# Three of the last quarter's four down units by seven block products, with adding DMAs for side and weight sums

## The chip, the cores and the metric

The kernel runs on one core of a Trainium2 chip. A core has a matrix engine (TensorE, PE in the profile; its weight loads are listed as PEld), a vector engine (VectorE, DVE), a scalar engine (ScalarE, ACT), a general engine (GpSimd, POOL) and SyncE (SP), which issues most DMAs. Matrix products are accumulated in PSUM, which has eight banks of 128 x 512 float32 numbers; everything else lies in SBUF, 128 partitions wide. The metric is device microseconds of one execution, lower is better.

## The reference, cut to what matters

Two layers, each with a token mixer, an MLP with a squared ReLU, and a gated embedding. All is float32; SEQ is 512, D_MODEL 1024, D_FF 4096. The change touches the MLP alone:

```python
for i in range(DEPTH):
    hn = rmsnorm(h, norm_mix_g[i])
    h = h + mixer(hn, ...)                                   # even or odd layout
    hn = rmsnorm(h, norm_mlp_g[i])
    u = jnp.square(jax.nn.relu(hn @ w_mlp_up[i]))            # 512 x 4096
    h = h + u @ w_mlp_down[i]                                # 512 x 1024
    gate = jax.nn.sigmoid(rmsnorm(h, norm_ple_g[i]) @ w_ple_gate[i])
    h = h + (p[i] @ w_ple_proj[i]) * gate
return rmsnorm(h, final_norm_g)
```

## The kernel before

**Layout.** The hidden state is kept transposed, as eight tiles `h[0..7]` of 128 features x 512 tokens. Each float32 operand of a product is split into a high half in TensorE's reduced float32 format (float32r) and a low half that holds the rest; `mm3` (line 137) makes one product of three matmuls, high x high, low x high, high x low. A split is one copy on ScalarE (`wh`, `uh`, `hi`) and one subtraction on VectorE (`wl`, `ul`, `lo`).

**Order.** The code names engines and data, and a scheduling layer fixes each engine's order of instructions when the program is built, from its own estimates of when things are ready; it puts in the semaphores. At run time every engine follows its list strictly, so an instruction that waits holds up all that stand behind it on its engine. Each DMA that SP or POOL issues stands in that engine's list in the same way.

**The MLP.** `mlp` (line 704) cuts the 4096 hidden columns into four quarters (`ch`), and each quarter into four up units and four down units (`c`). An up unit, `up(ch, c)`, loads 1 MB of weights (`raw`, two buffers), splits them, makes two 128 x 512 products (48 matmuls of 512 columns), multiplies by the norm's factor and clips at zero on VectorE (line 720), squares on ScalarE (line 721), and splits the result. The result `u` holds the four blocks B11, B12 (under the name T3), B21, B22: two tiles of hidden columns by two halves of 256 tokens.

A down unit, `down(ch, c)`, makes the two tiles `h[2c]`, `h[2c+1]` from the quarter's 1024 hidden columns. For quarters 0 to 2 it works by Strassen's scheme in Winograd's form: the 2 x 2 blocks of weights and of activations are first summed (`T1`, `T2`, `T3`, `T4` from u in lines 724 to 729; the weight sums in lines 742 to 745, on VectorE), and seven block products take the place of eight: 7 x 4 x 3 = 84 matmuls of 256 columns. The weights arrive packed block by block (`_pack4`). Three of the seven products are added into `h` directly; the four others go to two side tiles per unit, `sides[c][0..1]`, which collect over the quarters; `side_sums(c)` (line 788) then adds them into `h` by eight VectorE additions of 256 columns.

The last quarter is different. Its up units split only the four plain blocks, and its four down units, `down_last(c)` (line 798), are classical: 48 matmuls of 512 columns each, one PSUM tile per output tile. `side_sums` stands between the last up units, ahead of all of them. When a `down_last` unit has added its tile, `nxt.done(k)` (class `Norm`, line 230) splits `h[k]` for the gate's product and adds its square into the running sum of the next norm (line 247, VectorE).

**Around it.** After the MLP the gate stage starts (`ple_t` in layer 0, `ple_final` in layer 1); its first unit takes `h[0]` to `h[7]` in this order, and `ple_final` also transposes `h` back (line 858) and copies the result out of PSUM on VectorE (line 859). POOL has no work in the MLP.

The functions that the change touches follow.

Of the kernel before, what the change touches and what calls it, by code (L numbers as in the profile page):

```python
# [19 lines left out]
P = 128  # L20
# [42 lines left out]
def trunk(  # L63
# [139 lines left out]
    sbmask = const([P, P], "sbmask", F32R)  # L203
    nc.vector.tensor_copy(sbmask, mask)
    ident_r = const([P, P], "ident_r", F32R)
    nc.vector.tensor_copy(ident_r, ident)


# [21 lines left out]
    class Norm:  # L230
        def __init__(self, kind, layer):
            self.kind, self.layer, self.hl, self.acc = kind, layer, {}, None

        def done(self, k, stats=True):
            self.hl[k] = split_tile(h[k], gcol(self.kind, self.layer, k))
            if stats:
                self.stats(k)

        def stats(self, k, after=()):
            sq = t2k("e" if self.acc else "rstd")  # L240
# [461 lines left out]
    def mlp(layer, fpool, norm, nxt):  # L702
        ahl = norm.parts()
        rstd = []
        NCH = 4
        sides = [[fpool.tile([P, S], F32, tag=f"side{x}{c}", name=nm("side"), bufs=1) for x in range(2)] for c in range(4)]
        hidden = {}

        def up(ch, c):
            blk = block(w_up[layer, 4 * ch + c], KT, P)  # L710
            accs = [ps_wide() for _ in range(2)]
            run(lin_units(accs, blk, ahl, 0, KT, ch == 0 and c == 0))
            if not rstd:
                rstd.append(norm.finish(use_tables(sig_tail) if layer == 0 else None))
            u = fpool.tile([P, 7, HW], F32, tag="u", name=nm("u"), bufs=1)
            uh = fpool.tile([P, 7, HW], F32R, tag="uh", name=nm("uh"), bufs=5)
# [5 lines left out]
            parts = slice(0, 7)  # L722
            if ch < NCH - 1:
                nc.vector.tensor_tensor(
                    u[:, T1:T3 + 1:2], u[:, B11:B22 + 1:3], u[:, T3:T3 + 1].to_broadcast([P, 2, HW]), op=ALU.subtract)
                nc.vector.scalar_tensor_tensor(
                    u[:, T2], u[:, T1], -1.0, u[:, B22], op0=ALU.mult, op1=ALU.subtract)
                nc.vector.scalar_tensor_tensor(  # L728
                    u[:, T4], u[:, T2], -1.0, u[:, B21], op0=ALU.mult, op1=ALU.subtract)
            else:  # L730
                parts = slice(B11, B22 + 1)
            nc.scalar.activation(uh[:, parts], u[:, parts], AF.Copy)  # L732
            nc.vector.tensor_tensor(ul[:, parts], u[:, parts], uh[:, parts].bitcast(F32), op=ALU.subtract)  # L733
            hidden[ch, c] = (uh, ul)

        def down(ch, c):
            raw = wload(w_down[layer, 4 * ch + c])
            rv = raw.rearrange("p (s k c) -> p s (k c)", s=4, k=4)
            A12, A22, S3, A11 = range(4)
            sums = fpool.tile([P, 3, S], F32, tag="sums", name=nm("sums"), bufs=1)  # L740
            S1, S2, S4 = range(3)
            nc.vector.tensor_tensor(sums[:, S1], rv[:, S3], rv[:, A22], op=ALU.add)
            nc.vector.tensor_tensor(sums[:, S2], sums[:, S1], rv[:, A11], op=ALU.add)
            nc.vector.tensor_tensor(rv[:, S3], rv[:, S3], rv[:, A11], op=ALU.add)
            nc.vector.tensor_tensor(sums[:, S4], sums[:, S2], rv[:, A12], op=ALU.add)

            def split(src):
                n = src.shape[1]
                if n == 2:
                    hi, lo = (wpool.tile([P, 2, 4, P], F32R, tag=t, name=nm(t), bufs=3) for t in ("wh", "wl"))  # L750
                else:
                    hi, lo = (t2k("e", dtype=F32R).rearrange("p (s k c) -> p s k c", s=1, k=4) for _ in range(2))
                src = src.rearrange("p s (k c) -> p s k c", k=4)
                nc.scalar.activation(hi, src, AF.Copy)  # L754
                nc.vector.tensor_tensor(lo, src, hi.bitcast(F32), op=ALU.subtract)
# [5 lines left out]
            def product(bank, half, w, x, t, start, stop):  # L761
                wh, wl = w
                acc = banks[bank][:, half * HW:half * HW + HW]
                for k, (uh, ul) in enumerate(us):
                    mm3(acc, wh[:, x, k], wl[:, x, k], uh[:, t], ul[:, t], start and k == 0, stop and k == 3)

            def total(x, bank):
                if ch == 0:
                    nc.scalar.activation(sides[c][x], banks[bank], AF.Copy)
                else:  # L770
                    nc.vector.tensor_tensor(sides[c][x], sides[c][x], banks[bank], op=ALU.add)

            w = split(sums[:, S1:S2 + 1])
            product(0, 0, w, 0, T1, True, False)
            product(0, 1, w, 1, T2, False, True)
            total(0, 0)
            w = split(rv[:, S3:A11 + 1])
            product(1, 0, w, 0, T3, True, False)
            product(1, 1, w, 1, B11, False, True)
            total(1, 1)  # L780
            product(2, 1, split(sums[:, S4:S4 + 1]), 0, B22, True, False)
            w = split(rv[:, A12:A22 + 1])
            product(2, 0, w, 0, B21, False, True)
            nc.vector.tensor_tensor(h[2 * c], h[2 * c], banks[2], op=ALU.add)
# [3 lines left out]
        def side_sums(c):  # L788
            left, right = slice(0, HW), slice(HW, S)
            (s1t1, s2t2), (s3t3, a11b11) = ((x[:, left], x[:, right]) for x in sides[c])  # L790
            h11, h12, h21, h22 = (h[2 * c + i][:, x] for i in range(2) for x in (left, right))
            for dst, x, op in ((h11, a11b11, ALU.add), (s2t2, a11b11, ALU.add), (h12, s2t2, ALU.add), (s3t3, s2t2, ALU.add),
                               (h21, s3t3, ALU.subtract), (h12, s1t1, ALU.add), (s3t3, s1t1, ALU.add),
                               (h22, s3t3, ALU.subtract)):
                nc.vector.tensor_tensor(dst, dst, x, op=op)

        def down_last(c):
            blk = block(w_down[layer, 4 * (NCH - 1) + c], KT, P)
            uhl = [tuple(x[:, B11 + 2 * i:B11 + 2 * i + 2].rearrange("p a c -> p (a c)") for x in hidden[NCH - 1, k])
                   for k in range(4) for i in range(2)]  # L800
            for i in range(2):
                acc = ps_wide()
                lin(acc, blk[i][0], blk[i][1], uhl, 0, KT)
                nc.vector.tensor_tensor(h[2 * c + i], h[2 * c + i], acc, op=ALU.add)
                nxt.done(2 * c + i)
# [12 lines left out]
        for c in range(4):  # L818
            down_last(c)


    def ple_proj(layer, pool):
# [142 lines left out]
def _feeds(a):  # L965
# [3 lines left out]
    for layer, w in enumerate((a["w_in_even"][0], a["w_in_odd"][0])):  # L969
        blocks = []  # L970
        for j, g in enumerate(GROUPS[layer]):
# [4 lines left out]
            else:  # L976
# [20 lines left out]
        "w_down": np.array([[_pack(down[l], range(8 * ch, 8 * ch + 8), 256 * c, 256, 2) if ch == 3 else  # L997
                             _pack4(down[l], 8 * ch, 256 * c) for ch in range(4) for c in range(4)] for l in layers]),
        "w_gate": np.array([[_pack(gate[0], all8, 256 * c, 256, 2) for c in range(4)],
                            [_pack(gate[1], range(4 * hf, 4 * hf + 4), 512 * c, 512, 2, True)  # L1000
# [29 lines left out]
```

## Time and profile before

| | |
|---|---|
| median of 3 runs | 1310.03 us (1309.86 to 1310.09) |
| the profiled execution's own time | 1308.87 us |
| its span, first to last instruction | 1307.1 us |
| mean granted TensorE clock | 0.998 |
| busy: PE, DVE, ACT, POOL | 98%, 74%, 52%, 15% of the span |
| the last quarter in layer 0 | up units 1 to 3 from 541.4 us to 574.1, classical down units to 618.9 |
| the last quarter in layer 1 | classical down units from 1201.9 us to 1246.7 |

The page gives busy time by engine and by groups of instructions; the groups carry the mean duration of one instruction and the idle time before it, with what ended that idle time. A table by stretches of time (windows) tells which engine is full where. For matmuls the duration counts until the result has left the array, while the next one already runs, so what one matmul costs is read from the starts in the timeline. Times in the text are from the span's start.

### The profile page before, as it was taken

Reading aid. Unit: us, or ns where it says so; the run is one execution under the profiler, and the core shown is the slowest. Engines: PE = TensorE matmul, PEld = TensorE weight load, DVE = VectorE, ACT = ScalarE, POOL = GpSimd, SP = SyncE. Lnnn points to the kernel's source line nnn. Section 1 sums busy time; section 2 is a strip of 40 time slices with the busy share of each in tenths; the row PEclk is TensorE's granted clock in tenths of the full one; section 3 lists DMA queues with packets and bytes.
Section 4 is the critical chain, followed back from the end, with each engine's and each line's share of the span. In section 5 each row is a group of like instructions: output and inputs, shape, how many; then the busy total and the mean of one; then the engine's idle time right before and its main releaser. Section 6 shows DMA issues by size and latency. Waiting matters only on the chain.

```text
span 1307.1 us, 18561 instructions
## 1 busy us (share of the span) xinstructions
PE 1283.7 (98%) x7256; PEld 1117.4 (85%) x7256; DVE 973.5 (74%) x1623; ACT 686.0 (52%) x1117; POOL 189.8 (15%) x160
## 2 busy tenths in 40 slices
PE   9999999999999999999999999999999999999997
PEld 7988787888998989988889888788899898998876
DVE  7788888778848869845767877887784885994566
ACT  6666768554535334333456666765553443533344
POOL 2433434410000000000024333222000000000001
PEclk9999999999999999999999999999999999999999
DMA  6421423223232322323432222212223123232241
GB/s 217 135 81 50 140 93 115 89 82 112 86 108 97 102 92 97 129 97 101 157 112 96 84 89 78 69 57 95 99 97 124 70 97 129 73 122 97 97 145 65
DMA packets 28040, 133.20 MB, mean 102 GB/s; under 512 B 3312, under 2 KB 4048, under 8 KB 15280
## 3 DMA queue, kind: packets, MB, share of 16 engines
q1 hardware_dynamic: 27952, 132.01, 29.5%
q8 instruction: 57, 0.93, 0.3%
q14 instruction: 31, 0.25, 0.1%
HBM read 125.63 MB, written 6.37 MB: 101 GB/s over the span
## 4 chain that ended last, share of the span: by engine, by line
PE 85%; DVE 8%; ACT 4%; issue 1%; DMA 1%; SPq 0%; POOL 0%; ACTq 0%; DVEq 0%; POOLq 0%
PE mm L138 10%; PE mm L141 10%; PE mm L142 10%; PE sc L141 6%; PE sc L142 6%; PE sc L138 6%; PE pv L142 5%; PE pv L141 5%; PE pv L138 5%; PE tp L141 5%; PE tp L142 5%; PE tp L138 5%; PE pv L551 2%; PE tp L532 2%; PE sc L506 1%
## 5 line engine op out<-in xcount | busy, mean ns | idle before, releaser
L122 ACT ACTIVATE wh<-raw 128x1024 fp32r<-128x1024 f32 (+1 forms) x168 | 173.4, 1036 | 226.9 <-PE mm L141 63.0
L126 POOL TENSOR_TENSOR wl<-raw,wh 128x512 fp32r<-128x512 f32 (+1 forms) x132 | 177.1, 1364 | 309.3 <-ACT wh L122 303.6
L138 PE MATMUL mm<-hi,wh 128*128 128x512 f32 x472 | 187.0, 396 | 0.6 <-DVE v L443 0.4
L142 PE MATMUL mm<-hi,wl 128*128 128x512 f32 x472 | 184.8, 392 | 0.1
L141 PE MATMUL mm<-lo,wh 128*128 128x512 f32 x472 | 184.6, 391 | 0.0
L128 DVE TENSOR_TENSOR wl<-raw,wh 128x1024 fp32r<-128x1024 f32 x102 | 124.5, 1224 | 41.3 <-ACT wh L122 34.8
L142 PEld LDWEIGHTS mm<-hi,wl 128*128 128x128 f32 x472 | 88.6, 188 | 20.1 <-POOL wl L126 0.5
L138 PEld LDWEIGHTS mm<-hi,wh 128*128 128x128 f32 x472 | 88.7, 188 | 17.3 <-DVE v L443 0.6
L141 PEld LDWEIGHTS mm<-lo,wh 128*128 128x128 f32 x472 | 88.7, 188 | 15.6
L526 ACT ACTIVATE e<-e,mn 128x128 f32<-128x128 f32 (+3 forms) x96 | 53.8, 561 | 65.4 <-DVE mn L523 65.0
L754 ACT ACTIVATE wh<-raw 128x1024 fp32r<-128x1024 f32 x48 | 50.7, 1057 | 69.6 <-PE tp L141 35.1
L733 DVE TENSOR_TENSOR ul<-u,uh 128x1792 fp32r<-128x1792 f32 (+1 forms) x32 | 58.4, 1824 | 23.4 <-ACT uh L732 23.4
L732 ACT ACTIVATE uh<-u 128x1792 fp32r<-128x1792 f32 (+1 forms) x32 | 49.4, 1544 | 48.9 <-DVE u L728 48.7
L138 PE MATMUL sc<-hi,wh 128*128 128x512 f32 x184 | 71.9, 391 | 0.9 <-ACT hi L182 0.9
L141 PE MATMUL sc<-lo,wh 128*128 128x512 f32 x184 | 72.1, 392 | 0.3 <-DVE lo L183 0.3
L142 PE MATMUL sc<-hi,wl 128*128 128x512 f32 x184 | 71.8, 390 | 0.0
L721 ACT ACTIVATE u<-u 128x512 f32<-128x512 f32 x64 | 39.4, 625 | 53.8 <-DVE u L720 53.8
L142 PE MATMUL pv<-uh,wl 128*128 128x256 f32 (+1 forms) x224 | 67.4, 301 | 0.0
L142 PE MATMUL sc<-uh,wl 128*128 128x256 f32 (+1 forms) x224 | 67.3, 301 | 0.0
L141 PE MATMUL pv<-ul,wh 128*128 128x256 f32 (+1 forms) x224 | 67.2, 300 | 0.0
L141 PE MATMUL sc<-ul,wh 128*128 128x256 f32 (+1 forms) x224 | 67.2, 300 | 0.0
L138 PE MATMUL pv<-uh,wh 128*128 128x256 f32 (+1 forms) x224 | 66.6, 297 | 0.0
(259 smaller groups left out, 3645.4 us busy)
## 6 DMA issues: line engine op xcount, KB each, us to landing
raw<-in_w_up_dram SPq DMA_DIRECT2D x32, 1024.0 KB, 4.9
raw<-in_w_down_dram SPq DMA_DIRECT2D x32, 1024.0 KB, 4.9
raw<-in_w_in_dram SPq DMA_DIRECT2D x23, 1024.0 KB, 4.9
raw<-in_w_gate_dram SPq DMA_DIRECT2D x8, 1024.0 KB, 5.0
bias<-urow SPq DMA_DIRECT2D x24, 256.0 KB, 3.9
raw<-in_w_outa_dram SPq DMA_DIRECT2D x8, 768.0 KB, 4.2
pj<-pjd SPq DMA_DIRECT2D x16, 256.0 KB, 5.0
h<-in_xT_dram SPq DMA_DIRECT2D x8, 256.0 KB, 5.6
```

Source lines behind the costliest of these rows:

```text
L122: nc.scalar.activation(hi, src, AF.Copy)
L126: nc.gpsimd.tensor_tensor(lo[:, kx], src[:, kx], hi[:, kx].bitcast(F32), op=ALU.subtract)
L128: nc.vector.tensor_tensor(lo, src, hi.bitcast(F32), op=ALU.subtract)
L138: mm = nc.tensor.matmul(acc, lh, rh, start=start, stop=False)
L141: nc.tensor.matmul(acc, lh, rl, start=False, stop=False)
L142: nc.tensor.matmul(acc, ll, rh, start=False, stop=stop)
L526: nc.scalar.activation(e[:, 0:n], e[:, 0:n], AF.Exp, scale=-1.0, bias=mn, accum_out=s)
L532: nc.tensor.transpose(tp[:, j * P:(j + 1) * P], e[:, j * P:(j + 1) * P], ident)
L721: nc.scalar.activation(ui, ui, AF.Square, scale=0.5)
L732: nc.scalar.activation(uh[:, parts], u[:, parts], AF.Copy)
L733: nc.vector.tensor_tensor(ul[:, parts], u[:, parts], uh[:, parts].bitcast(F32), op=ALU.subtract)
L754: nc.scalar.activation(hi, src, AF.Copy)
```

## The change

The change makes units 0, 1 and 2 of the last quarter by the same seven block products as the earlier quarters, and unit 3 alone stays classical. In detail:

- The up units of the last quarter make the block sums too, so all seven blocks are split. Since T3 is overwritten with B22 - B12 while the classical unit needs B12, its high and low halves are first copied out (`b12`): into a small tile and, to save room, the second half of the `masks` tile for unit 0, and into a fifth buffer of `uh` (`spare`) for units 1 to 3.
- `down` now stores its weight sums in `s13` and `s24` and splits both, with A11, ahead of the first product. The four products of the first two banks are listed before the other three. In the last quarter's unit 0 they run over three of the four hidden pairs first and then the fourth.
- In the last quarter `s13` (S1 = A21 + A22 and S3 = A21 + A11) isn't added on VectorE: SP loads A21 twice from DRAM into `s13` (256 KB each), and POOL then issues a DMA of 512 KB that adds A22 and A11 to it in flight. `s13` has one buffer, so the first of these DMAs for the next unit waits until this unit's split has read it.
- In the last quarter the side products go from PSUM to a staging tile (ScalarE) and are added to `sides` by DMAs that POOL issues (256 KB each, two per unit).
- `side_sums(c)` for c = 0 to 2 moves behind the unit that follows unit c, together with the splits and squares of `h[2c]`, `h[2c+1]`; three of the squares are added to the norm's sum by DMAs of POOL as well.
- The classical unit reads B11 and B12 as two matmuls of 256 columns each, B21 and B22 as one of 512.
- `wide_i[0] = 0` starts the gate stage at the same PSUM bank as before.

```diff
-        def done(self, k, stats=True):
+        def done(self, k, stats=True, dma=None):
             self.hl[k] = split_tile(h[k], gcol(self.kind, self.layer, k))
             if stats:
-                self.stats(k)
+                self.stats(k, dma=dma)
...
+            elif dma is not None:
+                nc.gpsimd.dma_start(self.acc, sq, accum_op=ALU.add)
...
+            if ch == NCH - 1:
+                hi, lo = b12[c]
+                nc.scalar.activation(hi, u[:, T3], AF.Copy)
+                nc.vector.tensor_tensor(lo, u[:, T3], hi.bitcast(F32), op=ALU.subtract)
+            nc.vector.tensor_tensor(
+                u[:, T1:T3 + 1:2], u[:, B11:B22 + 1:3], u[:, T3:T3 + 1].to_broadcast([P, 2, HW]), op=ALU.subtract)
...
+            nc.scalar.activation(uh, u, AF.Copy)
+            nc.vector.tensor_tensor(ul, u, uh.bitcast(F32), op=ALU.subtract)
...
         def down(ch, c):
-            raw = wload(w_down[layer, 4 * ch + c])
+            src = w_down[layer, 4 * ch + c]
+            raw = wload(src)
...
+            s13 = fpool.tile([P, 2, S], F32, tag="s13", name=nm("s13"), bufs=1)
+            s24 = fpool.tile([P, 2, S], F32, tag="s24", name=nm("s24"), bufs=1)
+            if last:
+                sv = src.rearrange("p (s c) -> p s c", s=4)
+                for x in range(2):
+                    nc.sync.dma_start(s13[:, x], sv[:, A21])
+                nc.gpsimd.dma_start(s13, sv[:, A22:A11 + 1:2], accum_op=ALU.add)
...
+            nc.vector.tensor_tensor(s24[:, 0], s13[:, 0], rv[:, A11], op=ALU.add)
+            nc.vector.tensor_tensor(s24[:, 1], s24[:, 0], rv[:, A12], op=ALU.add)
...
+            def collect(dst, src, sign=1.0):
+                t = stage[0][:, stage[1]:stage[1] + src.shape[-1]]
+                stage[1] += src.shape[-1]
+                nc.scalar.activation(t, src, AF.Copy, scale=sign)
+                nc.gpsimd.dma_start(dst, t, accum_op=ALU.add)
...
+            w13, w24, w11 = split(s13), split(s24), split(rv[:, A11:A11 + 1])
+            for ks in ((0, 1, 2), (3,)) if last and c == 0 else (range(4),):
+                product(0, 0, w13, 0, T1, True, False, ks)
+                product(0, 1, w24, 0, T2, False, True, ks)
+                product(1, 0, w13, 1, T3, True, False, ks)
+                product(1, 1, w11, 0, B11, False, True, ks)
             total(0, 0)
             total(1, 1)
+            product(2, 1, w24, 1, B22, True, False)
             w = split(rv[:, A12:A22 + 1])
             product(2, 0, w, 0, B21, False, True)
             nc.vector.tensor_tensor(h[2 * c], h[2 * c], banks[2], op=ALU.add)
             product(3, 0, w, 1, T4, True, True)
             nc.vector.tensor_tensor(h[2 * c + 1][:, 0:HW], h[2 * c + 1][:, 0:HW], banks[3][:, 0:HW], op=ALU.subtract)
+            if last and c:
+                finished(c - 1)
...
+        def finished(c):
+            side_sums(c, low)
+            for i in range(2):
+                nxt.done(2 * c + i, dma=sides[c][i] if c < 2 else None)
...
             for c in range(1, 4):
                 up(ch, c)
-                if ch == NCH - 1:
-                    side_sums(c)
-        side_sums(0)
-        for c in range(4):
-            down_last(c)
+        side_sums(3)
+        for c in range(3):
+            down(NCH - 1, c)
+        down_last(3)
+        wide_i[0] = 0
```

The next two pieces show where the change moves instructions. The names carry the numbers that the program gives its buffers; lines are those of the kernel that the piece belongs to.

**VectorE, around up unit 3 of the last quarter, layer 0.** Before, this is the stretch from the first clipping (`u_5617<-pv_5567`, the unit's first product) to the first classical unit:

```order
L720 SCALAR_TENSOR_TENSOR u_5617<-pv_5567,rstd_2957 128x512
L128 TENSOR_TENSOR wl_5649<-raw_5642,wh_5648 128x1024
L720 SCALAR_TENSOR_TENSOR u_5617<-pv_5568,rstd_2957 128x512
L128 TENSOR_TENSOR wl_5720<-raw_5717,wh_5719 128x1024
L733 TENSOR_TENSOR ul_5619<-u_5617,uh_5618 128x1024
L804 TENSOR_TENSOR h_94<-h_94,mm_5652 128x512
```

Now, from the same clipping to the split of the unit's seven blocks (`s_1005` and `s_1006` are unit 1's `s13` and `s24`, `wl_5742` the low half of unit 0's last two blocks of weights, `spare_5481` the low half of B12):

```order
L729 SCALAR_TENSOR_TENSOR u_5629<-pv_5579,rstd_2956 128x512
L761 TENSOR_TENSOR s_1006_5774<-s_1005_5773,raw_5771 128x512
L762 TENSOR_TENSOR s_1006_5774<-s_1006_5774,raw_5771 128x512
L734 TENSOR_TENSOR spare_5481<-u_5629,spare_5481 128x256
L729 SCALAR_TENSOR_TENSOR u_5629<-pv_5580,rstd_2956 128x512
L772 TENSOR_TENSOR wl_5742<-raw_5651,wh_5741 128x1024
L735 TENSOR_TENSOR u_5629<-u_5629 128x2x256
L737 SCALAR_TENSOR_TENSOR u_5629<-u_5629 128x256
L739 SCALAR_TENSOR_TENSOR u_5629<-u_5629 128x256
L742 TENSOR_TENSOR ul_5631<-u_5629,uh_5630 128x1792
```

Unit 1's weight sums, which need its adding DMA, now stand between the two clippings of up unit 3.

**POOL, the MLP of layer 0.** Before there is nothing. Now, in this order (`s_989`, `s_1005` and `s_1026` are the `s13` of units 0, 1 and 2; `side_3067` to `side_3070` are the side tiles of units 0 and 1):

```order
L757 DMA s_989_5653<-in_w_down_dram 128x2x512
L757 DMA s_1005_5773<-in_w_down_dram 128x2x512
L794 DMA side_3067<-stage_5664 128x512
L794 DMA side_3068<-stage_5664 128x512
L757 DMA s_1026_5913<-in_w_down_dram 128x2x512
L794 DMA side_3069<-stage_5784 128x512
L794 DMA side_3070<-stage_5784 128x512
```

Unit 2's weight DMA stands behind the two side DMAs of unit 0 and ahead of those of unit 1.

More of the change, by code (lines that the diff above doesn't have):

```diff
@@ L706, in mlp @@
         sides = [[fpool.tile([P, S], F32, tag=f"side{x}{c}", name=nm("side"), bufs=1) for x in range(2)] for c in range(4)]
-        hidden = {}
+        hidden, spare, stages, b12, low = {}, [], [], [], []
         def up(ch, c):
@@ L745, in down @@
-            nc.vector.tensor_tensor(sums[:, S4], sums[:, S2], rv[:, A12], op=ALU.add)
+            A12, A22, A21, A11 = range(4)
+            last = ch == NCH - 1
+            s13 = fpool.tile([P, 2, S], F32, tag="s13", name=nm("s13"), bufs=1)
[5 more added lines that the diff above has]
+                nc.gpsimd.dma_start(s13, sv[:, A22:A11 + 1:2], accum_op=ALU.add)
+            else:
+                nc.vector.tensor_tensor(s13[:, 0], rv[:, A21], rv[:, A22], op=ALU.add)
+                nc.vector.tensor_tensor(s13[:, 1], rv[:, A21], rv[:, A11], op=ALU.add)
@@ L786, in down, with down_last, side_sums @@
             nc.vector.tensor_tensor(h[2 * c + 1][:, 0:HW], h[2 * c + 1][:, 0:HW], banks[3][:, 0:HW], op=ALU.subtract)
-        def side_sums(c):
+            if last and c:
+                finished(c - 1)
+        def down_last(c):
+            blk = block(w_down[layer, 4 * (NCH - 1) + c], KT, P)
+            low.clear()
+            finished(c - 1)
+            for i, (wh, wl) in enumerate(blk):
+                acc = ps_wide()
+                for m in range(4):
+                    uh, ul = hidden[NCH - 1, m]
+                    bh, bl = b12[m]
+                    for r, rows in enumerate((((acc[:, 0:HW], uh[:, B11], ul[:, B11]), (acc[:, HW:S], bh, bl)),
+                                              ((acc, *(x[:, B21:B22 + 1].rearrange("p a c -> p (a c)") for x in (uh, ul))),))):
+                        k = 2 * m + r
+                        for lh, x in ((wh, 1), (wh, 2), (wl, 1)):
+                            for row in rows:
+                                nc.tensor.matmul(row[0], lh[:, k], row[x], start=k == 0 and x == 1 and lh is wh and row is rows[0],
+                                                 stop=k == KT - 1 and lh is wl)
+                nc.vector.tensor_tensor(h[2 * c + i], h[2 * c + i], acc, op=ALU.add)
+                nxt.done(2 * c + i)
+        def finished(c):
+            side_sums(c, low)
+            for i in range(2):
+                nxt.done(2 * c + i, dma=sides[c][i] if c < 2 else None)
+        def side_sums(c, after=()):
             left, right = slice(0, HW), slice(HW, S)
@@ L794, in side_sums @@
                                (h22, s3t3, ALU.subtract)):
[L795 to L805, printed above, removed]
+                ins = nc.vector.tensor_tensor(dst, dst, x, op=op).ins
+                for a in after:
+                    order(ins, a)
         for c in range(4):
@@ L996, in _feeds @@
         "w_up": np.array([[_pack(up[l], all8, 256 * c, 256, 2) for c in range(16)] for l in layers]),
[L997 removed]
+        "w_down": np.array([[_pack(down[l], range(8 * ch, 8 * ch + 8), 256 * c, 256, 2) if (ch, c) == (3, 3) else
                              _pack4(down[l], 8 * ch, 256 * c) for ch in range(4) for c in range(4)] for l in layers]),
```

59 lines of the change are left out of this document (26 added, 33 removed).

## The prediction

> **What bounds the kernel now.** I read the page first, then the table by stretches around the last quarter, then the timeline of the matmuls. The page:
>
> ```profile
> span 1307.1 us, 18561 instructions
> PE 1283.7 (98%) x7256; PEld 1117.4 (85%) x7256; DVE 973.5 (74%) x1623; ACT 686.0 (52%) x1117; POOL 189.8 (15%) x160
> ...
> PEclk9999999999999999999999999999999999999999
> ...
> PE 85%; DVE 8%; ACT 4%; issue 1%; DMA 1%; SPq 0%; POOL 0%; ACTq 0%; DVEq 0%; POOLq 0%
> ```
>
> TensorE is busy throughout, at full clock, and carries 85% of the chain that ended last. The question is whether this holds in the stretch that changes. The windows of layer 0 are one Strassen unit with its surroundings, the last quarter's up units 1 to 3, its four classical down units, and of layer 1 the start of the gate stage:
>
> ```profile
> core 0: us, PE busy (x) PEld busy (x) DVE busy (x) ACT busy (x) POOL busy (x), PEclk, DMA share, GB/s
> 531.30:541.40 10.10, 10.10 (x87) 10.10 (x86) 10.06 (x21) 3.19 (x3) 0.00 (x0) 1.00 0.37 117
> 541.40:574.10 32.70, 32.70 (x147) 27.05 (x146) 15.81 (x21) 11.29 (x14) 0.00 (x0) 1.00 0.32 111
> 574.10:618.90 44.80, 44.80 (x194) 36.05 (x193) 24.81 (x30) 18.00 (x25) 0.00 (x0) 1.00 0.28 96
> ...
> 1246.70:1256.00 9.30, 8.15 (x49) 6.22 (x48) 9.10 (x14) 5.55 (x7) 0.00 (x0) 1.00 0.83 274
> ```
>
> In the last quarter TensorE never stops, so fewer matmul columns there would shorten the run one for one, as long as the weights and activations arrive in time. VectorE has room (24.81 of 44.80 us), but a quarter's last Strassen unit has it full (10.06 of 10.10), and the start of the gate stage loses 1.15 us of TensorE to it. What a matmul costs is read from the starts in the timeline:
>
> ```profile
> 529.75 0.28 PE L142 MATMUL tp<-uh,wl 128*128 128x256 f32 x1
> 529.87 0.28 PE L138 MATMUL tp<-uh,wh 128*128 128x256 f32 x1
> ...
> 531.31 0.28 PE L138 MATMUL pv<-uh,wh 128*128 128x256 f32 x1
> ...
> 541.39 0.39 PE L138 MATMUL sc<-hi,wh 128*128 128x512 f32 x1
> ...
> 574.07 0.40 PE L138 MATMUL mm<-uh,wh 128*128 128x512 f32 x1
> ...
> 618.87 0.39 PE L138 MATMUL mm<-hi,wh 128*128 128x512 f32 x1
> ```
>
> A matmul of 256 columns starts 0.120 us after the one before. The last Strassen unit runs from 531.31 to 541.39, 10.08 us for 84. The three up units take 32.68 us for 144 matmuls of 512 columns, 10.9 us a unit, 0.227 each; the four classical down units 44.80 us for 192, 11.20 a unit, 0.233 each.
>
> **Term 1, the matmuls.** Three units go from 11.20 to 10.08 us. The last unit now has 24 matmuls of 512 columns (5.60 us) and 48 of 256 (5.76): 11.36 us. 3 x 10.08 + 11.36 = 41.60 against 44.80, **3.20 us a layer less, 6.4 in all**. This needs TensorE to be fed.
>
> **Term 2, VectorE behind up unit 3.** Unit 0 needs up unit 3's blocks, and the work ahead of them has grown. Durations:
>
> ```profile
> L755 DVE TENSOR_TENSOR wl<-raw,wh 128x1024 fp32r<-128x1024 f32 x48 | 58.6, 1221 | 9.1 <-ACT wh L754 9.0
> ...
> L754 ACT ACTIVATE wh<-raw 128x1024 fp32r<-128x1024 f32 x48 | 50.7, 1057 | 69.6 <-PE tp L141 35.1 <-PE mm L141 18.6 <-issue 9.1
> ...
> L733 DVE TENSOR_TENSOR ul<-u,uh 128x1792 fp32r<-128x1792 f32 x24 | 48.6, 2024 | 19.8 <-ACT uh L732 19.8
> ...
> L732 ACT ACTIVATE uh<-u 128x1792 fp32r<-128x1792 f32 x24 | 40.9, 1704 | 48.7 <-DVE u L728 48.7
> ...
> L742 DVE TENSOR_TENSOR sums<-raw 128x512 f32<-128x512 f32 x24 | 16.5, 689 | 2.1 <-DMA raw<-in_w_down_dram 1.9
> ...
> L795 DVE TENSOR_TENSOR h<-h,side 128x256 f32<-128x256 f32 x40 | 16.1, 421 | 0.1
> ```
>
> Back to back, VectorE starts the next instruction some 0.08 us before the last one's end, as these three starts (0.60 apart, duration 0.68) show:
>
> ```profile
> 342.35 0.68 DVE L742 TENSOR_TENSOR sums<-raw 128x512 f32<-128x512 f32 x1
> 342.95 0.68 DVE L784 TENSOR_TENSOR h<-h,tp 128x512 f32<-128x512 f32 x1
> 343.55 0.68 DVE L743 TENSOR_TENSOR sums<-sums,raw 128x512 f32<-128x512 f32 x1
> ```
>
> So an instruction of 256, 512, 1024 or 1792 columns costs 0.34, 0.60, 1.14 or 1.94 us. Time 0 is the end of up unit 2's matmuls. VectorE clips (0.2 to 0.8), waits for ScalarE's copy of `s13` (1.06), makes unit 0's first low half (ends at 2.5), then B12's low half, three subtractions with 0.1 us of dependency before each, and a single-block split (5.2). It waits for ScalarE's 1.70 us copy of up unit 2's blocks (6.2), subtracts (8.2), makes another low half (9.4) and clips (10.0). There stand unit 1's weight sums, to which term 3 returns. Without a wait: two sums, B12's low half and a clipping to 12.3, a low half to 13.4, three subtractions to 15.1, ScalarE's copy to 16.8. TensorE finishes up unit 3 at 10.9 and has 45 matmuls of the first three hidden pairs, 5.4 us: it stops at 16.3. That is 0.5 us of waiting, and 0.5 more for the low half (1.94 us) against 13 matmuls (1.56). With 0.2 for the first low half of unit 1: **1.2 us a layer**. The bounds are 0, if the sums of many small dependencies come out 1 us shorter, and 2.
>
> **Term 3, the adding DMA of the weights.** No DMA in this trace is issued by POOL, none adds. The nearest rows, with KB and median microseconds from issue to landing, and the spread of the 256 KB loads called `bias`:
>
> ```profile
> raw<-in_w_down_dram SPq DMA_DIRECT2D x32, 1024.0 KB, 4.9
> ...
> bias<-urow SPq DMA_DIRECT2D x24, 256.0 KB, 3.9
> ...
> raw<-in_w_outa_dram SPq DMA_DIRECT2D x8, 768.0 KB, 4.2
> ...
> raw<-in_pT_dram SPq DMA_DIRECT2D x2, 512.0 KB, 3.9
> ...
> DMA to landing us min/median/max: 3.0/3.9/6.5
> ```
>
> Call A the time of the 512 KB adding DMA from issue to landing. Its chain is serial: the split of the last unit's `s13` must be done, two loads of 256 KB land (3.0 alone, 0.3 for the second issue: 3.4), then A. For unit 1 the split ends at 2.5, so the DMA is issued at 6.2, and VectorE asks for its result at 10.0: a wait of A - 3.8, and all of term 2 behind it, the fourth hidden pair first, is late by as much. For unit 2 the split ends 0.5 us into unit 1, the DMA starts at 4.4, and ScalarE (1.06) and VectorE (1.22) follow. TensorE needs them at 10.08 and 10.3: a wait of A - 3.6, and 0.4 more for the second pair of sums. Together a layer waits 1.2 + (A - 3.8) + (A - 3.6) + 0.4 = 2A - 5.8 us, where A is above 3.8.
>
> A's lower bound is a plain load of the size, 3.9, or the quickest 256 KB, 3.0, below which nothing more is won. The upper bound is a DMA that reads the source first and then the target, twice 3.9. As it reads 1024 KB and writes 512, I take the load of 768 KB, **A = 4.2: 2.6 us a layer**. Each further 0.1 us of A costs 0.4 us.
>
> The Trainium skill (DMA: Bandwidth & Descriptors, Anatomy of one DMA) fits a DMA that GpSimd issues by 2.0 us plus its bytes at 436 GB/s. That is an estimate of 3.2 us here, under which A costs nothing and the time would be 1304.4. The row of the plain 512 KB load, 3.9 us, is already above the fit's value for the same bytes, so it gets no more than a share of the quick end.
>
> **Term 4, what else moves.** The side DMAs (256 KB) are asked for by VectorE only one unit later, some 10 us, behind weights that are needed sooner; at the 3.9 us of their nearest row they cost nothing, and they would cost what they exceed about 6 us by. The eight additions of each `side_sums` (8 x 0.34 = 2.7 us) move from the up units behind the next unit, where VectorE has 10.08 us a unit for about 9.5 of work; that is the cover, and it is thin. ScalarE's two extra copies a unit lie in its free half. In layer 1 the gate stage's first low half of weights now comes ahead of the third transposed copy on VectorE:
>
> ```profile
> L858 PE MATMUL tp<-ident,h 128*128 128x128 f32 x32 | 4.9, 277 | 0.6 <-DVE ht L859 0.6
> ...
> L141 PE MATMUL mm<-wl,hi 128*128 128x512 f32 x4 | 1.8, 441 | 0.5 <-DVE wl L128 0.5
> ```
>
> These two waits, 1.1 us, and some 0.5 us of slow starts beside them (441 ns against 390) go: **1.6 us once**, between 0 and 1.8.
>
> **The sum.** -6.4 + 2 x 2.6 - 1.6 = -2.8 us. The profiled execution took 1308.87 us, 1.8 more than its span, and would take 1306.1; the median of the three runs shown is 1.16 higher, and the forecast against it is **1307.2 us**.
>
> **Rivals.** *The adding DMA is slow.* One mechanism, at POOL's weight DMA for units 1 and 2: the target is read as well as the source, and in unit 2 the 1 MB load for unit 3 (4.9 us) starts about when the adding DMA does and shares the engines. From A = 5.6 on the kernel is slower by more than 0.2%. At 6.5 a layer waits 7.2 us, the sum is -6.4 + 14.4 - 1.6 = +6.4 and the time 1316.4; at 7.8 it is 1321.6. For it: a 256 KB load has taken up to 6.5 us in company. Against: the DMA engines are at 0.28 in this stretch. By the Trainium skill (the same page, Issuing engines are not separate DMA queues) POOL's DMAs run on the engines that SP's use and interleave with them; that speaks for the sharing, and no row here shows it for POOL. *The gain is eaten exactly.* A between 4.3 and 5.6, where waits and columns cancel: at 4.9, the row of 1 MB, a layer waits 4.0, the sum is 0.0 and the time 1310.0. *The DMAs hide.* A below 3.8: only term 2 stays, 1.2 a layer, -6.4 + 2.4 - 1.6 = -5.6, 1304.4. *The change doesn't save columns,* because weight loads set the pace of short matmuls: the 84 of an existing unit at 0.120 us speak against it, and it has no share.
>
> **How the numbers follow.** About 0.2%, 2.6 us, is what a measurement of this kernel can tell from no change. The forecast and its neighbours, with A from 3.8 to 4.3, have 0.30; the DMAs hide, 0.12: faster 0.42. Eaten exactly 0.25: same. Slow DMA 0.33: slower. The range goes from 1303.5, hidden DMAs with term 2 near half, to 1317.5, A at 6.8. The likeliest case's own range, A from 3.8 to 4.3, is 1305.6 to 1307.6.
>
> **What would show it.** Strassen units of 84 matmuls 0.120 us apart and a mixed unit of 11.4 show term 1. A wait of TensorE for ScalarE's `uh` in unit 0 of about 0.9 us (0.5 + A - 3.8), then for `ul`, shows term 2. VectorE idle before the first `s24` sum (line 761) released by POOL's DMA shows A in unit 1, and TensorE idle for `wh` and `wl` at the start of unit 2 shows it there; the time to landing of line 757 gives A itself. I am wrong if A is above 5, if VectorE waits for side DMAs at line 852, or if the last unit's matmuls don't keep 0.12 and 0.23.

## The result, and the profile after

The changed kernel takes 1327.59 us (1326.57 to 1330.1) against 1309.94 us of the kernel before, four runs each: 17.65 us more, ratio 1.0138 with a 95% interval of 1.012 to 1.0155. The forecast was 1307.2 us, the range ended at 1317.5: the kernel is slower where it was forecast faster, and by more than the range allowed. The profiled execution took 1330.1 us with a span of 1328.3, 21.2 more than before. The page of the changed kernel:

```profile
span 1328.3 us, 19332 instructions
PE 1286.5 (97%) x7520; PEld 1134.2 (85%) x7520; DVE 1006.4 (76%) x1673; ACT 711.6 (54%) x1149; POOL 212.0 (16%) x184
...
PEclk9999999999999999988999999999999999999899
...
PE 79%; DVE 9%; ACT 5%; DMA 3%; issue 3%; SPq 0%; POOL 0%; ACTq 0%; DVEq 0%; POOLq 0%
```

TensorE is busy for as long as before although it has fewer columns to do, its clock is no longer full in two places, and DMAs and "issue" now hold 6% of the chain. The two places are the last quarter's down units of the two layers. The table by stretches, of layer 0, goes from up unit 3's end to the wait in unit 0, that wait, what follows it, then unit 1, the wait at the start of unit 2, and what follows that:

```profile
core 0: us, PE busy (x) PEld busy (x) DVE busy (x) ACT busy (x) POOL busy (x), PEclk, DMA share, GB/s
573.00:579.20 6.20, 6.20 (x49) 6.01 (x48) 1.20 (x3) 2.00 (x3) 0.00 (x0) 1.00 0.44 77
579.20:585.00 5.80, 0.36 (x4) 0.15 (x2) 3.91 (x8) 2.33 (x2) 0.00 (x0) 0.71 0.40 134
585.00:588.40 3.40, 3.40 (x16) 3.40 (x17) 1.94 (x1) 0.63 (x1) 0.00 (x0) 0.50 0.19 80
...
591.40:601.40 10.00, 9.98 (x84) 9.77 (x83) 7.23 (x14) 3.77 (x6) 3.53 (x4) 1.00 0.92 229
601.40:606.00 4.60, 0.76 (x5) 0.35 (x3) 2.33 (x3) 2.32 (x4) 0.00 (x0) 0.94 1.01 184
606.00:612.30 6.30, 6.06 (x28) 6.06 (x29) 6.15 (x12) 1.76 (x2) 0.86 (x1) 0.50 0.42 83
```

Unit 1 does its 84 matmuls in 10 us, as forecast. Ahead of it and behind it TensorE stands still, and after each standstill it runs at half clock: 16 matmuls in 3.40 us and 28 in 6.06, 0.21 us each in place of 0.12. Starts in the timeline show the same thing one by one:

```profile
579.09 0.28 PE L141 MATMUL sc<-ul,wh 128*128 128x256 f32 x1
579.21 0.29 PE L142 MATMUL sc<-uh,wl 128*128 128x256 f32 x1
584.93 0.79 PE L138 MATMUL mm<-uh,wh 128*128 128x256 f32 x2 [5.44 <-ACT uh L741]
...
586.16 0.41 PE L142 MATMUL sc<-uh,wl 128*128 128x256 f32 x1
586.38 0.41 PE L138 MATMUL sc<-uh,wh 128*128 128x256 f32 x1
...
604.79 0.39 PE L138 MATMUL mm<-uh,wh 128*128 128x256 f32 x1 [3.13 <-ACT wh L771]
```

What TensorE waited for in layer 1's last quarter (engine and line, what it waited for, us in total, times, longest):

```profile
PE mm L138 <- ACT uh L741: 4.6, 1, 4.6
PE mm L138 <- ACT wh L771: 3.8, 1, 3.8
PE mm L142 <- DVE wl L772: 0.7, 1, 0.7
```

The account of the span goes by the starts of the matmuls. From the first down matmul to the first of the gate stage, layer 0 takes 573.93 to 630.13, 56.2 us, where it took 44.8. The columns alone would take 41.6, as forecast. A start that comes later than 0.12 us (256 columns) or 0.233 us (512) after the one before is late by the rest. Where the timeline shows a wait, these rests sum to 10.2 us: the waits. Where it shows none, they sum to 4.6 us: the half clock. Layer 1 has 9.9 and 4.1 and takes 55.3 us. (The parts add up to within 0.3 us.) The start of the gate stage in layer 1 gains 1.3 us, and in layer 1's mixer a wait of 1.3 us that was there before is now followed by half clock, 0.7 us net. Together 11.4 + 10.5 - 1.3 + 0.7 = 21.3, the 21.2 of the span. The median lies 2.5 us under the profiled execution; which of these parts is smaller in the other executions no trace shows.

Where the waits come from, the engines' timelines tell: SP's two loads of A21 for unit 1, POOL's adding DMA, VectorE's first use of its result; then the same three for unit 2:

```profile
565.50 0.80 SPq L756 DMA_DIRECT2D s<-in_w_down_dram  x2
...
570.55 1.09 POOL L757 DMA_DIRECT2D s<-in_w_down_dram  x1 [35.61 <-DMA s<-in_w_down_dram]
...
578.08 0.69 DVE L761 TENSOR_TENSOR s<-s,raw 128x512 f32<-128x512 f32 x1 [4.97 <-issue]
...
591.75 0.82 SPq L756 DMA_DIRECT2D s<-in_w_down_dram  x2
...
597.92 1.07 POOL L757 DMA_DIRECT2D s<-in_w_down_dram  x1 [5.83 <-DVE side L852]
...
603.63 0.69 DVE L761 TENSOR_TENSOR s<-s,raw 128x512 f32<-128x512 f32 x1 [3.04 <-DMA s<-in_w_down_dram]
```

From the first load to the use it is 12.6 us for unit 1 and 11.9 for unit 2. (The releasers "issue" and "side" are the page's guesses; the landing of the DMA falls together with the use each time.) The groups of DMA issues, and the spreads of the two loads (line 756) and of the adding DMA (line 757):

```profile
s<-in_w_down_dram SPq DMA_DIRECT2D x12, 256.0 KB, 4.1
s<-in_w_down_dram POOLq DMA_DIRECT2D x6, 512.0 KB, 6.6
side<-stage POOLq DMA_DIRECT2D x12, 256.0 KB, 4.7
...
DMA to landing us min/median/max: 3.5/4.1/5.8
...
DMA to landing us min/median/max: 5.7/6.6/8.7
```

A, the quantity on which the forecast hung, has a median of 6.6 us over all six and is never under 5.7, where 4.2 was taken. The four DMAs of units 1 and 2, the only ones that VectorE waited for, took 7.45 and 5.69 us in layer 0, 5.69 and 5.76 in layer 1.

### The profile page after: what moved, and what is told of

It reads as the page before. It is cut to its first block, busy times and chain, and to the rows that moved or that the text cites. A ratio compares the mean times of both kernels' runs of the same rounds, so it can differ in the third digit from the quotient of the medians.

```text
span 1328.3 us, 19332 instructions
## 1 busy us (share of the span) xinstructions
PE 1286.5 (97%) x7520; PEld 1134.2 (85%) x7520; DVE 1006.4 (76%) x1673; ACT 711.6 (54%) x1149; POOL 212.0 (16%) x184
## 4 chain that ended last, share of the span: by engine, by line
PE 79%; DVE 9%; ACT 5%; DMA 3%; issue 3%; SPq 0%; POOL 0%; ACTq 0%; DVEq 0%; POOLq 0%
PE mm L138 11%; PE mm L142 11%; PE mm L141 10%; PE sc L138 5%; PE sc L141 5%; PE sc L142 5%; PE pv L142 4%; PE pv L141 4%; PE pv L138 4%; PE tp L141 4%; PE tp L142 4%; PE tp L138 3%; PE pv L553 2%; PE tp L534 2%; DMA s<-in_w_down_dram 2%
## 5 line engine op out<-in xcount | busy, mean ns | idle before, releaser
L122 ACT ACTIVATE wh<-raw 128x1024 fp32r<-128x1024 f32 (+1 forms) x156 | 160.6, 1034 | 147.3 <-PE mm L141 50.9
L128 DVE TENSOR_TENSOR wl<-raw,wh 128x1024 fp32r<-128x1024 f32 x90 | 109.7, 1222 | 49.9 <-ACT wh L122 43.6
L757 POOL DMA_DIRECT2D s<-in_w_down_dram x6 | 6.7, 1112 | 616.6 <-DMA s<-in_w_down_dram 338.7
L771 ACT ACTIVATE wh<-s 128x1024 fp32r<-128x1024 f32 x60 | 63.2, 1053 | 59.5 <-DVE s L760 14.7
L742 DVE TENSOR_TENSOR ul<-u,uh 128x1792 fp32r<-128x1792 f32 x32 | 64.8, 2024 | 30.7 <-ACT uh L741 30.6
L772 DVE TENSOR_TENSOR wl<-s,wh 128x1024 fp32r<-128x1024 f32 x60 | 73.3, 1221 | 13.0 <-ACT wh L771 12.6
L741 ACT ACTIVATE uh<-u 128x1792 fp32r<-128x1792 f32 x32 | 54.5, 1703 | 50.6 <-DVE u L739 50.6
L138 PE MATMUL mm<-uh,wh 128*128 128x256 f32 x192 | 57.4, 301 | 17.0 <-ACT uh L741 10.0
L138 PE MATMUL mm<-wh,hi 128*128 128x256 f32 (+1 forms) x216 | 63.2, 292 | 0.1
L142 PE MATMUL mm<-wh,lo 128*128 128x256 f32 (+1 forms) x216 | 63.0, 292 | 0.0
```

The costliest lines, as they stand in the source:

```text
L138: mm = nc.tensor.matmul(acc, lh, rh, start=start, stop=False)
L142: nc.tensor.matmul(acc, ll, rh, start=False, stop=stop)
L741: nc.scalar.activation(uh, u, AF.Copy)
L742: nc.vector.tensor_tensor(ul, u, uh.bitcast(F32), op=ALU.subtract)
L772: low[:] = [nc.vector.tensor_tensor(lo, src, hi.bitcast(F32), op=ALU.subtract).ins]
```

## The experiments

All ten kernels ran beside the kernel before; times are medians.

**1. The sums of s13 on VectorE.** In the last quarter as in the others:

```diff
-            if last:
-                ...
-                nc.gpsimd.dma_start(s13, sv[:, A22:A11 + 1:2], accum_op=ALU.add)
-            else:
-                nc.vector.tensor_tensor(s13[:, 0], rv[:, A21], rv[:, A22], op=ALU.add)
-                nc.vector.tensor_tensor(s13[:, 1], rv[:, A21], rv[:, A11], op=ALU.add)
+            nc.vector.tensor_tensor(s13[:, 0], rv[:, A21], rv[:, A22], op=ALU.add)
+            nc.vector.tensor_tensor(s13[:, 1], rv[:, A21], rv[:, A11], op=ALU.add)
```

> The changed kernel, but the last quarter's s13 is again added by VectorE (two additions of 512 columns a unit, 0.60 us each); the side sums keep their adding DMAs. Theory A, the serial chain of two loads and one adding DMA makes the waits: TensorE's waits of 5.4 us in unit 0 and of 3.1 and 0.95 us at the start of unit 2 (layer 0) shrink to what VectorE's list leaves, 1.2 to 2.8 us a layer, no matmul runs at half clock, and the time is 1305 to 1308 us. Theory B, the side sums' adding DMAs and VectorE's backlog behind them make the waits: the time stays above 1320 us.

Measured: 1310.77 us, ratio 1.0011 (1.0002 to 1.002). Of the 17.65 us some 16.5 are gone, so the chain of loads and adding DMA made them. In the last quarter TensorE now waits as term 2 of the prediction says:

```profile
PE mm L141 <- DVE ul L742: 0.7, 1, 0.7
PE mm L138 <- ACT uh L741: 0.4, 1, 0.4
```

But the forecast of this run, 1305 to 1308, failed too: at the start of layer 1's gate stage, where the change itself gained, this kernel lost. The timelines of TensorE, SP and VectorE there, and the spread of the side DMAs (line 788 in this kernel):

```profile
1245.74 0.66 PE L901 MATMUL tp<-ident,h 128*128 128x128 f32 x4 [1.20 <-DVE h L831]
1249.95 1.11 PE L901 MATMUL tp<-ident,h 128*128 128x128 f32 x4 [3.55 <-DVE h L831]
...
1228.60 4.61 SPq L114 DMA_DIRECT2D raw<-in_w_gate_dram  x2
...
1241.00 0.42 DVE L846 TENSOR_TENSOR side<-side,side 128x256 f32<-128x256 f32 x1 [4.38 <-DMA side<-stage]
...
DMA to landing us min/median/max: 3.4/5.8/11.1
```

The last side DMA of unit 2 was issued at 1229.92 and landed at 1240.97, 11.05 us later, with two 1 MB loads of gate weights in flight; VectorE stood 4.4 us before it, TensorE 4.8 us in two pieces, and half clock followed. Waits and slow starts there cost 5.3 us more than in the kernel before. So theory B was wrong for the change as it stands, and right for the next thing to become late.

**2. The side sums on VectorE**, s13 by DMA as in the change:

```diff
-                elif not last:
+                else:
                     nc.vector.tensor_tensor(sides[c][x], sides[c][x], banks[bank], op=ALU.add)
-                else:
-                    collect(sides[c][x], banks[bank])
...
-                nxt.done(2 * c + i, dma=sides[c][i] if c < 2 else None)
+                nxt.done(2 * c + i)
```

> The changed kernel, but the last quarter's side products and squares are added by VectorE, straight from PSUM; s13 keeps its loads and its adding DMA. Theory A: the waits stay, and the time is 1322 to 1328 us (the 256 KB loads of unit 2 no longer share the engines with side DMAs, up to 1.1 us a layer less). Theory B: the time falls to 1312 us or less.

Measured: 1326.9 us, ratio 1.0133 (1.0119 to 1.0147). The waits in layer 0 are 3.7, 2.8 and 0.8 us, the half clock 3.3. With the side DMAs gone the result is the same: they didn't make it.

**3. No adding DMA at all** (the edits of 1 and 2):

> Both undone: only the block products are left of the change, and VectorE makes all sums. If VectorE has room (it is busy 76% of the span), the time is that of the run with the sums on VectorE, within 1 us. If a unit's 10.1 us are full with about 9.5 us of VectorE's work, then two side additions (0.60 us each) and a square's addition more a unit make VectorE the bound in units 1 and 2: TensorE waits 2 to 4 us a layer more and the time is 1308 to 1315 us.

Measured: 1313.85 us, ratio 1.0031 (1.002 to 1.0043). VectorE's load does decide: a wait of 3.3 us in unit 2 of each layer, with VectorE busy for all of it, and half clock behind. These are windows on the wait and on what follows:

```profile
595.70:599.20 3.50, 0.22 (x3) 0.03 (x1) 3.50 (x7) 1.93 (x4) 0.00 (x0) 1.00 0.00 0
599.20:603.20 4.00, 4.00 (x21) 4.00 (x22) 3.43 (x5) 0.87 (x1) 0.00 (x0) 0.59 0.10 16
```

**4 and 5. What the DMA costs.** POOL's weight DMA without the addition, and the same plain DMA by SP:

```diff
-                nc.gpsimd.dma_start(s13, sv[:, A22:A11 + 1:2], accum_op=ALU.add)
+                nc.gpsimd.dma_start(s13, sv[:, A22:A11 + 1:2])     # run 4
+                nc.sync.dma_start(s13, sv[:, A22:A11 + 1:2])       # run 5
```

> The changed kernel, but POOL's weight DMA of 512 KB (line 757) overwrites s13 and adds nothing, so the computation lacks the sums S1 and S3; all else is as it was. If reading the target and adding is what makes this DMA slow (5.7 to 8.5 us from issue to landing), it falls to about 3.9 us, the plain 512 KB load of SP, the waits shrink by 2 to 3.5 us each and the time falls to 1312 to 1318 us. If the cost lies in POOL's way of issuing and in the shared engines, it stays at 5 us or more and the time above 1322 us.

> As the run before, but the DMA that overwrites s13 is issued by SP (S1 and S3 are missing again). By the row of the plain 512 KB load it lands after 3.9 to 4.5 us, and TensorE's waits become 5.4 - 3 = 2.4 us in unit 0 and 4.1 - 1.7 = 2.4 us in unit 2; with them the half clock goes, and the time is 1312 to 1317 us. If it is the two loads ahead and the sharing of the engines that hold the chain, the time stays above 1320 us.

Measured: 1320.66 us (ratio 1.0084, 1.0065 to 1.0102) and 1319.97 us (1.0078, 1.006 to 1.0097). The spread of the 512 KB DMA, POOL's and then SP's:

```profile
DMA to landing us min/median/max: 4.3/4.9/6.6
```

```profile
DMA to landing us min/median/max: 4.1/4.7/5.5
```

Run 4 leaves every engine's order as it was. Over all six DMAs the medians say that adding costs 1.7 us (6.6 against 4.9) and POOL in place of SP 0.2. The four that are waited for took 4.34, 4.90, 4.87 and 4.95 us without the addition, 3.1, 0.8, 0.8 and 0.8 us less than with it; why the first one lost so much more, no trace shows. Some 0.3 us of each difference is POOL's own issuing instruction (1.09 us against 0.75). The two profiled spans differ by 8.6 us, some 6.2 of it waits and 2.3 half clock. For 5.5 us less of DMA that is 1.1 us of wait for each us, where the prediction had one for each of the four DMAs. But both expectations were too hopeful by some 3 us: even a plain DMA leaves the change 10 us slower than before, since the two loads ahead of it take their 4.0 us and more, and waits of 1.5 to 3.4 us remain at all four places (two a layer). In run 4 each of them ends in half clock, in run 5 one of the four.

**6. Filling the wait of unit 2** with 16 matmuls whose result is cleared:

```diff
+            if last and c == 2:
+                idle(16, us, banks[3])      # 16 x matmul(bank[:, HW:S], uh[:, B11, 0:P], uh[:, B11])
```

> The changed kernel with 16 matmuls of 256 columns (1.9 us) put on TensorE's list ahead of unit 2 of the last quarter, into a bank that is cleared afterwards; they lie inside its wait of 4.1 us. If the half clock behind that wait (28 matmuls of 0.213 us in layer 0) comes from TensorE's idleness, the clock there stays full, the mean clock rises from 0.987 to 0.990 or more and the time falls by 2 to 4 us, to 1324 to 1326. If the clock falls for another reason, clock and time stay.

Measured: 1326.72 us, ratio 1.0127 (1.0112 to 1.0143), inconclusive: the waits of layer 0 are still 1.1, 0.9 and 0.7 us close together, and behind them 23 matmuls ran at half clock; the mean clock rose from 0.987 to 0.990 all the same. The extra matmuls also changed VectorE's order in unit 2, so the run changed two things. Experiment 10 repeats it where only one changes.

**7. The side additions on POOL**, no adding DMA:

```diff
-                ins = nc.vector.tensor_tensor(dst, dst, x, op=op).ins
+                ins = eng.tensor_tensor(dst, dst, x, op=op).ins     # eng is POOL for units 0 to 2
```

> The block products with no adding DMA at all: VectorE makes the weight sums and collects the side products, and POOL, which is idle in the MLP, does the eight additions of each side_sums of units 0 to 2. Where nothing added by DMA, TensorE waited 3.3 us for VectorE in unit 2; POOL takes 8 x 0.34 = 2.7 us a unit from VectorE. If VectorE's load is all that is left, the waits are those of term 2 alone (1.1 to 1.5 us in unit 0, under 1 in unit 2), none long enough for the half clock, and the time is 1305 to 1308 us, faster than before. If POOL's additions slow VectorE or come too late for the gate stage, it is 1311 us or more.

Measured: 1314.85 us, ratio 1.0041 (1.0028 to 1.0053). Taking 2.7 us a unit from VectorE did not shorten the run. TensorE's wait of 3.3 us in unit 2 became two of 1.6 and 0.9, but others came in their place: 0.7 us more in layer 0's unit 2, and 1.6 us where layer 1's gate stage starts. The two engines slow each other; the instructions of single lines (ns, min/median/max, first and last start) show it. VectorE's low halves in this kernel:

```profile
L766 DVE TENSOR_TENSOR wl<-raw,wh x30: 1215/1224/1758, 335.7 to 1236.2; 128x1024 fp32r<-128x1024 f32 x30
```

The same in the kernel of experiment 3:

```profile
L766 DVE TENSOR_TENSOR wl<-raw,wh x30: 1214/1219/1226, 335.1 to 1232.0; 128x1024 fp32r<-128x1024 f32 x30
```

And POOL's additions:

```profile
L844 POOL TENSOR_TENSOR h<-h,side x30: 726/1064/1722, 586.7 to 1249.7; 128x256 f32<-128x256 f32 x30
```

A low half takes up to 1.76 us in place of 1.22, and POOL's additions 0.73 to 1.72 us. The Trainium skill (SBUF — State Buffer, Who interferes with whom) says that a VectorE instruction with two SBUF inputs and a GpSimd instruction that reads SBUF contend for one read interface; both are of that kind here, and the trace agrees.

**8 and 9. Two block units, no adding DMA**, once between the classical units and once ahead of them. The weights of the classical units are packed plainly, and their `side_sums` stand between the last up units. Run 8, in which the first classical unit takes three of the four hidden pairs for both of its tiles before the fourth:

```diff
-        side_sums(3)
-        for c in range(3):
-            down(NCH - 1, c)
+        down_last(0)
+        down(NCH - 1, 1)
+        down(NCH - 1, 2)
         down_last(3)
```

Run 9:

```diff
-        side_sums(3)
-        for c in range(3):
+        for c in range(2):
             down(NCH - 1, c)
+        down_last(2)
         down_last(3)
```

> No adding DMA; of the last quarter only units 1 and 2 are made by block products, unit 0 and unit 3 stay classical, and unit 0 takes three of the four hidden pairs for both of its tiles first. Saved a layer: 2 x (11.20 - 10.08) less 2 x 0.16 for the split matmuls of the mixed form, 1.9 us. Unit 0 now has three quarters of 11.36 us, 8.5 us, of matmuls before it needs up unit 3, in place of 5.4 us, which covers the waits of 0.4 and 0.7 us; units 1 and 2 have a classical unit on either side, in which VectorE can catch up. If VectorE's load was what remained, no wait is left and the time is 2 x 1.9 = 3.8 us below before, 1305 to 1307 us. If VectorE fills up again by the second block unit, as it did by the third when nothing added by DMA (3.3 us), the time is 1309 us or more.

> The same count of matmuls as the run before, in the order of the change: units 0 and 1 by block products, units 2 and 3 classical, no adding DMA. The waits for up unit 3 in unit 0 stay (0.4 and 0.7 us, with the slow starts beside them 1.5 us a layer), nothing else: 2 x (1.9 - 1.5) = 0.8 us below before, 1308 to 1310 us. If it is as quick as the run with unit 0 classical (within 1 us), the place of the classical unit doesn't matter.

Measured: 1304.73 us, ratio 0.9961 (0.9948 to 0.9973), and 1307.26 us, 0.998 (0.9971 to 0.9989). Both are faster than before; with a classical unit first it is 5.1 us, more than the 3.8 expected, the best of all. (The profiled executions differ by 3.6; where the rest comes from, no trace shows.) The whole last quarter of run 8, in both layers:

```profile
573.44:616.46 43.02, 42.93 (x313) 40.39 (x312) 39.29 (x62) 22.31 (x30) 0.00 (x0) 1.00 0.28 98
1200.07:1243.09 43.02, 42.94 (x313) 40.38 (x312) 37.76 (x60) 20.45 (x28) 0.00 (x0) 1.00 0.28 97
```

43.02 us a layer against 44.80, at full clock, with 0.25 us of waits. VectorE is busy for 39.29 of 43.02 us; with a third block unit's sums beside that TensorE waited 3.3 us a layer (experiment 3). Run 9 had been expected at 1308 to 1310 us. It keeps the waits of 0.4 and 0.7 us in unit 0, takes 44.27 us in layer 0 where run 8 takes 43.02, and is 2.5 us slower, which is two layers of that.

**10. Filling the wait of experiment 3** with 24 matmuls, all else in its place:

```diff
                 product(0, 0, w13, 0, T1, True, False, ks)
+                if last and c == 2:
+                    idle(24, us, banks[3])
```

> The kernel without any adding DMA (three block units, 1313.85 us), with 24 matmuls of 256 columns (24 x 0.12 = 2.9 us) put on TensorE's list in unit 2 at the place where it waited 3.28 us for VectorE's weight sums; they write a bank that is cleared afterwards, and no other engine's list changes. If TensorE's idleness brings the half clock behind that wait (some 18 matmuls of 0.213 us, 1.8 us a layer), the clock stays full there and the time falls by 2 x 1.8 = 3.6 us, to 1310 to 1311 us, though the wait for VectorE is as it was. If the half clock has another cause, the time stays at 1313 to 1315 us.

Measured: 1311.0 us, ratio 1.001 (1.0001 to 1.0019), against 1313.85 and 1.0031 without the 48 matmuls, whose work is of no use. The same two stretches as in experiment 3:

```profile
595.60:599.20 3.60, 3.60 (x32) 3.60 (x32) 3.60 (x8) 2.04 (x5) 0.00 (x0) 1.00 0.00 0
599.20:603.20 4.00, 3.58 (x30) 3.38 (x30) 4.00 (x5) 1.99 (x2) 0.00 (x0) 1.00 0.00 0
```

The clock stays at 1.00 and 30 matmuls fit where 21 did. The half clock comes from TensorE's own idleness.

## Why the prediction was wrong, step by step

- **Term 1, the matmuls: right.** 84 matmuls 0.12 us apart in unit 1, 41.6 us of columns in each layer. The rival that weight loads set the pace was rightly given nothing.
- **Term 2, VectorE behind up unit 3: right in kind, at the upper bound in size.** 1.2 us a layer was forecast, 2 at most; with the DMA out of the way (experiment 1) the waits of layer 0 are 0.4 and 0.7 us, and with the slow starts beside them some 2 us.
- **Term 3, the chain of the weight DMA: the step that failed.** Its structure held: in layer 0 the loads for unit 1 were issued at 565.50, 2.5 us after up unit 2's end, and VectorE asked at 573.1, 10.1 us after it, both to 0.1 us as written. Two sizes in it did not hold.
  - *A itself.* It was taken as 4.2 from the load of 768 KB. The four DMAs that were waited for took 7.45, 5.69, 5.69 and 5.76 us, 7.8 more in all than four times 4.2. The bounds held for these four (3.9, and 7.8 for a source read and then a target; the two of unit 0, which nothing waited for, took 8.5 and 8.7). The choice between the bounds did not: a row of a plain load says nothing of a DMA that reads its target, and the value should have stood in the middle of the range.
  - *The way to A.* From the issue of the first load to POOL's start the prediction has 3.7 us for unit 1 and 3.9 for unit 2: 3.4 for the two loads, from the quickest row, and 0.3 and 0.5 that it doesn't explain. Measured are 5.1 and 6.2 in layer 0, 6.0 and 6.8 in layer 1, 8.8 us more in all. The second load landed 4.5 us after the first's issue for unit 1 of layer 0 (at 569.96) and 5.4 to 6.2 us after it in the three other chains, those of unit 2 beside side DMAs and a 1 MB load, and POOL started 0.6 us after the second landed each time.

  So the loads ahead were missed by at least as much as A. With the measured A of units 1 and 2 the formula 2A - 5.8 gives 7.3 us of waits for layer 0 and 5.7 for layer 1 in place of 2.6; measured are 10.2 and 9.9, and the longer way, 3.6 us in layer 0 and 5.2 in layer 1, more than covers the rest. Both layers together wait 20.1 us in place of 5.2.
- **A step that was missing: a wait costs more than its length.** The prediction took each wait at its own length. Behind each long one TensorE ran at half clock, 4.6 and 4.1 us in the two layers. This alone would have made 1315.9 us of the forecast, still inside the range; the 14.9 us of longer waits alone make 1322.1, beyond it. The slow-DMA rival had the right mechanism, place and sign, with a chance of 0.33, but priced A = 6.5 at 1316.4, without the longer way to A and without the half clock.
- **Term 4: half right.** The side DMAs cost the change nothing, as forecast (experiment 2), though VectorE waits 3.8 us for two of them:

```profile
L852 DVE TENSOR_TENSOR h<-h,side 128x256 f32<-128x256 f32 x40 | 16.2, 421 | 4.1 <-DMA side<-stage 3.8
```

The bound of about 6 us was the right place to look: when the chain was taken away, one took 11.05 us and the gate stage paid (experiment 1). The gain at that stage, 1.6 us forecast, came as 1.3. The cover called thin, VectorE's 9.5 of 10.08 us, is what stops the version without DMAs (experiment 3).

## What to carry to other kernels

A DMA whose result is waited for within a unit of work is a chain, not a price: count the loads ahead of it at their times in company, the issuing engine's start, and the landing, and give an operation that no row shows the middle of its bounds, not the nearest friendly row. Where TensorE is the bound, a wait costs more than its length: behind one of 2.2 us or more came 1.4 to 2.8 us of half clock here, as much as one or two of the saved block products (12 matmuls, 1.44 us). When an engine is the cover, look first for an order that lets it catch up (here a classical unit on either side of the block units), and only then for a slower engine or a DMA to take its work.

## What the runs showed of the hardware

- **Half clock after idleness.** Every wait of TensorE of 2.2 us or more in the last quarters of these runs was followed by 14 to 28 matmuls of 256 columns at 0.213 us; lone waits up to 0.75 us never were. Waits of 1 to 2.1 us, or several close together that sum to 2 to 3.5, sometimes were: 1.6 and 0.9 us in experiment 7 in layer 1, not in layer 0; not 2.05, 0.99 and 0.21 us in layer 0 of experiment 5. In layer 1's mixer the same two waits, 1.3 and 0.5 us, are followed by half clock in the changed kernel and not in the kernel before. The Trainium skill (TensorE: Matmul & The Clock Gate, What's actually happening) has the clock fall after an idle window of about 3.4 us and come back after a busy one of the same length, with windows that run freely. The slow stretch of 3.40 us in unit 0 agrees, while the one of 6.06 us in unit 2 is longer; the fall after a wait of 2.36 us (experiment 4, layer 0) is earlier than that. What decides in the cases between stays open.
- **An adding DMA of 512 KB** took 5.7 to 8.7 us (median 6.6), the plain one by POOL 4.3 to 6.6 (4.9), by SP 4.1 to 5.5 (4.7).
- **A 256 KB adding DMA** took 3.3 us at the quickest and up to 11.1 beside two loads of 1 MB.
- **POOL and VectorE side by side**: 1.22 us became up to 1.76 on VectorE, 0.73 up to 1.72 on POOL.
